# Merge gates ahead of the units in seven products of quarters, token-major projections, FoX heads begun after q and k

## The chip, the cores and the metric

One core of a Trainium2 chip runs the whole layer. The metric is the device time of one execution in microseconds, median of the runs. The engines are TensorE (matmuls and transposes, PE in the profile), VectorE (DVE), ScalarE (ACT), GpSimd (POOL) and SyncE (SP), which issues most DMAs.

## What is computed

The layer takes 512 tokens of width 2048 (float32) through an RMS norm and one wide input product, two branches, and a gated merge:

```
h = rmsnorm(x, norm_gain)
u = h @ w_in                                    # 2048 -> 12488 columns
q, k, v, z_a, f_logit | r, kr, vr, z_b, w, a | g_a, g_b = split(u)
o_a = fox_attention(q, k, v, cumsum(log_sigmoid(f_logit + bias))) * silu(z_a)   # 8 heads of 128
o_b = (rwkv7(shifted r, kr, vr, w, a) + bonus) * silu(z_b)                      # 16 heads of 64
m   = sigmoid(g_a) * (o_a @ w_proj_fox) + sigmoid(g_b) * (o_b @ w_proj_rwkv)    # 1024 -> 2048 each
out = rmsnorm(x + m @ w_out, final_norm_gain)
```

The two gates g_a and g_b are 2 x 2048 of the columns of u. The matrix products must hold float32 accuracy.

## The kernel before

Every large product is made of three matmuls in the float32r type: each operand is split into a high part (a cast, on ScalarE) and a low part (what the cast left, a subtraction on VectorE), and high x high, high x low and low x high are added up in PSUM. The normed input is kept transposed, as `hhi` and `hlo`, 16 blocks of 128 channels by 512 tokens.

`u_tile` (L292) makes one tile of 128 columns of u by 512 tokens: `product` (L278) runs over 16 blocks of 128 input channels, with a 128x128 piece of the weights stationary and 512 tokens moving, 48 matmuls in all. The weights come in pieces of 256 KB: `load_raw` (L236) issues the load on SyncE into one of four `raw` buffers, `split_pieces` (L254) makes `whi` (L266, ScalarE) and `wlo` (L267, VectorE), `next_piece` (L242) keeps both ahead of the matmuls. All pieces stand in one list in the order of use.

TensorE and SyncE run in the order in which the code emits; the other engines are ordered by the framework's scheduler from priorities. The order on TensorE comes from a main generator (`stage1`, L855) that emits the weight tiles, and workers that it spawns (`fox_head`, `rwkv_front`, `rwkv_chain` and others): after each matmul of the main generator a virtual clock in `mm` (L127) advances, and workers whose due time has come (the table `LAG`) put their small matmuls in between. So heads and chains of the recurrence ride in the gaps of the weight tiles.

The stages are, in time: the norm and the transposed input with the first tile `wd` (to 35 us), `ad` (to 47 us), the units (60 tiles, 47 to 897 us: per pair of RWKV heads the tiles k, r, z, v, each evacuated by `shift`, L443, and from the second pair on one FoX head with q, k, v, z and `fox_head`, L776), then the merge: 32 gate tiles `g` and 32 projection tiles `p` (24 matmuls each), with `p` three tiles behind `g`, and FoX head 7 between the first three `g` and the first `p` (L317 to L330, L910 to L942). The gate goes through a tanh on ScalarE into one of four `sg` buffers; after the projection VectorE forms (tanh + 1) x p and adds the second branch's product to the first's in `m_all`. `mhi` and `mlo` (L945 to L947) are its parts, channel-major, and serve the out stage (L1003 on) as stationary operand with 512 columns of w_out moving. The branches' outputs go through DRAM (`oa_d`, `ob_d`) and come back as `oraw`.

## Time and profile before

| | |
|---|---|
| median of 3 runs | 1675.99 us (1674.42 to 1678.16) |
| the profiled execution | 1676.68 us |
| its span | 1674.8 us |
| mean granted TensorE clock | 0.993 |
| TensorE busy | 1628.9 us (97%), 8506 instructions |
| VectorE busy | 958.0 us (57%) |
| ScalarE busy | 710.4 us (42%) |
| GpSimd busy | 83.6 us (5%) |
| DMA | 170.24 MB, mean 102 GB/s |

The busy time of an engine is the union of its instructions; matmuls overlap, so the 0.39 us of one matmul is its latency, and the distance from one start to the next is its price on the engine. The table is of one execution; the stretches below tell where in it an engine was busy.

### The profile page before, as it was taken

The numbers are of one execution on the slowest core, as the hardware profiler recorded it, in microseconds if no ns is written. First come the engines' busy times: TensorE is split into PE (matmuls) and PEld (weight loads), VectorE is DVE, ScalarE is ACT, GpSimd is POOL, SyncE is SP. The second block draws the span as 40 slices with busy tenths as digits, with TensorE's granted clock in tenths as the row PEclk, the third lists the DMA queues.
The fourth block names the chain that finished last, engine by engine and source line by source line (L and its number), as shares of the span: only waits on it lengthen the run. The fifth ranks groups of instructions, "written<-read, shape, count | busy, mean of one in ns | idle before, by whom it ended". The sixth has DMA issues, their size and how long they took to land.

```text
span 1674.8 us, 23424 instructions
## 1 busy us (share of the span) xinstructions
PE 1628.9 (97%) x8506; PEld 1332.3 (80%) x8506; DVE 958.0 (57%) x2005; ACT 710.4 (42%) x1453; POOL 83.6 (5%) x149
## 2 busy tenths in 40 slices
PE   6998998999999999999999999999999999999998
PEld 6887876778878778788788788888888888888886
DVE  6468587786877777678668454222224333353432
ACT  7544354474464464553744444222223222243322
POOL 3010001000000000010000000000000000001110
PEclk9999998999999999999999999999999999999999
DMA  5342423333333324334334244335334333343422
GB/s 167 97 107 69 105 61 90 98 87 86 90 96 98 99 70 111 86 78 104 85 86 115 76 123 118 95 98 148 94 96 148 97 95 98 98 160 117 138 83 101
DMA packets 287978, 170.24 MB, mean 102 GB/s; under 512 B 38790, under 2 KB 270830, under 8 KB 287222
## 3 DMA queue, kind: packets, MB, share of 16 engines
q1 hardware_dynamic: 284358, 156.13, 35.4%
q0 software_dynamic: 2064, 9.46, 1.5%
q10 hardware_dynamic: 1440, 3.15, 0.5%
q8 instruction: 67, 1.10, 0.3%
q14 instruction: 49, 0.40, 0.1%
HBM read 158.19 MB, written 10.50 MB: 101 GB/s over the span
## 4 chain that ended last, share of the span: by engine, by line
PE 83%; DVE 9%; ACT 3%; issue 2%; DMA 2%; SPq 1%; POOL 0%; DVEq 0%; ACTq 0%; POOLq 0%
PE u_g L135 20%; PE p L135 11%; PE o L135 10%; PE u_fq L135 6%; PE u_fk L135 5%; PE u_z L135 4%; PE u_fv L135 4%; PE u_k L135 4%; PE u_fz L135 4%; PE u_v L135 4%; PE u_r L135 2%; DVE Wt L482 2%; DVE W L642 1%; PE sc L135 1%; PE y L135 1%
## 5 line engine op out<-in xcount | busy, mean ns | idle before, releaser
L135 PE MATMUL u_g<-hhi,wlo_g 128*128 128x512 f32 x512 | 200.6, 392 | 0.0
L135 PE MATMUL u_g<-hhi,whi_g 128*128 128x512 f32 x512 | 200.4, 391 | 0.0
L135 PE MATMUL u_g<-hlo,whi_g 128*128 128x512 f32 x512 | 200.0, 391 | 0.0
L267 DVE TENSOR_TENSOR wlo_g<-raw_g,whi_g 128x512 fp32r<-128x512 f32 x128 | 88.4, 690 | 169.8 <-ACT whi_g L266 167.6
L266 ACT ACTIVATE whi_g<-raw_g 128x512 fp32r<-128x512 f32 x128 | 80.9, 632 | 228.1 <-PE u_g L135 115.1
L135 PEld LDWEIGHTS u_g<-hlo,whi_g 128*128 128x128 f32 x512 | 96.2, 188 | 20.3
L135 PEld LDWEIGHTS u_g<-hhi,wlo_g 128*128 128x128 f32 x512 | 96.2, 188 | 20.2
L135 PEld LDWEIGHTS u_g<-hhi,whi_g 128*128 128x128 f32 x512 | 96.2, 188 | 19.7
L482 DVE TENSOR_TENSOR Wt<-W,Lt 128x16 f32<-128x16 f32 (+30 forms) x248 | 101.0, 407 | 5.6
L267 DVE TENSOR_TENSOR wlo_p<-raw_p,whi_p 128x512 fp32r<-128x512 f32 x64 | 44.3, 693 | 103.3 <-ACT whi_p L266 103.3
L135 PE MATMUL p<-ohi,whi_p 128*128 128x512 f32 x256 | 101.0, 394 | 0.0
L135 PE MATMUL p<-ohi,wlo_p 128*128 128x512 f32 x256 | 100.4, 392 | 0.0
L135 PE MATMUL p<-olo,whi_p 128*128 128x512 f32 x256 | 99.6, 389 | 0.0
L266 ACT ACTIVATE whi_p<-raw_p 128x512 fp32r<-128x512 f32 x64 | 40.4, 631 | 121.9 <-PE u_g L135 120.3
L135 PE MATMUL o<-whi_o,mhi 128*128 128x512 f32 x224 | 87.3, 390 | 0.1
L135 PE MATMUL o<-wlo_o,mhi 128*128 128x512 f32 x224 | 87.2, 389 | 0.0
L135 PE MATMUL o<-whi_o,mlo 128*128 128x512 f32 x224 | 87.1, 389 | 0.0
L267 DVE TENSOR_TENSOR wlo_o<-raw_o,whi_o 128x512 fp32r<-128x512 f32 x56 | 42.6, 762 | 76.2 <-ACT whi_o L266 75.9
L642 DVE TENSOR_REDUCE W<-Wt 128x8 f32<-128x16 f32 (+30 forms) x248 | 72.4, 292 | 5.6
L266 ACT ACTIVATE whi_o<-raw_o 128x512 fp32r<-128x512 f32 x56 | 35.3, 631 | 83.6 <-PE o L135 79.3
L135 PE MATMUL u_fq<-hhi,whi_fq 128*128 128x512 f32 x128 | 53.7, 419 | 5.2 <-DVE z L448 5.2
L719 ACT ACTIVATE pre<-SV,E 64x64 f32<-64x64 f32 x112 | 38.6, 345 | 46.3 <-DVE SV L732 45.4
(352 smaller groups left out, 3924.3 us busy)
## 6 DMA issues: line engine op xcount, KB each, us to landing
raw_g<-in_w_in_dram SPq DMA_DIRECT2D x128, 256.0 KB
raw_o<-in_w_out_dram SPq DMA_DIRECT2D x56, 256.0 KB
raw_k<-in_w_in_dram SPq DMA_DIRECT2D x32, 256.0 KB
raw_r<-in_w_in_dram SPq DMA_DIRECT2D x32, 256.0 KB
raw_z<-in_w_in_dram SPq DMA_DIRECT2D x32, 256.0 KB
raw_v<-in_w_in_dram SPq DMA_DIRECT2D x32, 256.0 KB
raw_fq<-in_w_in_dram SPq DMA_DIRECT2D x32, 256.0 KB
raw_fk<-in_w_in_dram SPq DMA_DIRECT2D x32, 256.0 KB
```

The source lines that it names most:

```text
L135: PE.matmul(out, lhsT=lhsT, rhs=rhs, start=start, stop=stop, **kw)
L266: S.activation(whi, raw, AF.Copy)
L267: V.tensor_tensor(wlo, raw, whi.bitcast(F32), ALU.subtract)
L482: eng.tensor_tensor(o, a, b, op)
L642: V.tensor_reduce(W[:, :, i], tmp[:, :, 0:i + 1], AX.X, ALU.add)
L719: S.activation(pre[hs[q]], SV[hs[q], c, q, :], AF.Copy, scale=E1[hs[q], c, CH:CH + 1])
```

## The change

The two gates are computed first, right behind the tile `ad`, and for all tokens: in four groups of 1024 columns (two per gate). A group is a product of the 512 x 2048 input with a 2048 x 1024 block of weights. Each is cut into four quarters, and seven products of sums of quarters take the place of eight products of quarters, as in Strassen's method in Winograd's form (`fast`). Products are now token-major: a 128 x 128 piece of the input or of one of four sums of its quarters is stationary and 512 columns of weights move. A group has 28 units (seven products by four blocks of 256 rows) of 12 matmuls, and each unit needs a weight operand of 128 x 1024. VectorE forms the weight differences (`prep`), and the sums of the products from PSUM; ScalarE casts and takes the tanh; the result is stored by GpSimd's queue in `sg_d` in DRAM, 2 x 512 x 2048. In the first group, products that need no sums come first (`seq0`), and `make_sums` builds the four sums of the input's quarters beside them, in four rounds with one buffer `st`: GpSimd adds high and low parts to get the quarter back, VectorE makes the sums and low parts, ScalarE the casts. Weight loads are 512 KB, in four buffers `gb`, on SyncE. The pools of this stage are closed before those of the units open.

The tiles of the units come in the order of `order`: k and r of a pair, then the four tiles of a FoX head, then z and v of the pair. A FoX head begins behind its k tile and takes v and z when they come; head 7 follows head 6. One entry of `LAG` (f5) goes from 16.0 to 12.5.

The projections come behind all units. They too are token-major: for each branch and each block of 512 columns, four banks (one per 128 tokens), eight pieces of weights moving. The gates are read back from `sg_d` (four loads of 256 KB per block). The merged rows are then token-major, so `turn_merged` turns them by 64 transposes on TensorE, in sets of four: a block of columns is turned during the next block of the second branch, the last one behind the last matmul. The out stage is the same.

```diff
-    units = [("rw", 0), ("rw", 1)]
-    for i in range(2, 8):
-        units += [("fox", i - 2), ("rw", i)]
-    units += [("fox", 6)]
...
-    for n in range(len(merge) + WIN):
-        if n == WIN:
-            add_unit("fox", 7)
-        if n < len(merge):
-            br, j, g0, wp = merge[n]
-            add_tile(f"g{br}_{j}", [(0, w_in[:, g0 + j * P:g0 + (j + 1) * P])])
-        if n >= WIN:
-            br, j, g0, wp = merge[n - WIN]
-            add_tile(f"p{br}_{j}", [(0, wp[:, j * P:(j + 1) * P])], nk=FW // P)
...
+    order = []
+    for i in range(NP):
+        order += [("rw", i, "k"), ("rw", i, "r")]
+        if i > 1:
+            order += [("fox", i - 2, nm) for nm in "qkvz"]
+        order += [("rw", i, "z"), ("rw", i, "v")]
+    order += [("fox", i, nm) for i in (6, 7) for nm in "qkvz"]
...
+    for br, wp in enumerate((w_proj_rwkv[0], w_proj_fox[0])):
+        for n in range(4):
+            for k in range(KB):
+                pieces.append((f"p{br}_{n}_{k}", [(0, wp[k * P:(k + 1) * P, n * 512:(n + 1) * 512])], 1, 512))
...
+        seq0 = [(p, j) for p in "1256743" for j in J]
+        seq = [(p, j) for j in J for p in "15"] + [("6", j) for j in J] + [("2", 0)] + [("7", j) for j in J]
+        seq += [("2", 1), ("4", 0), ("2", 2), ("4", 1), ("2", 3), ("4", 2), ("4", 3)] + [("3", j) for j in J]
+        units = [(g, p, j) for g in groups for p, j in (seq0 if g == groups[0] else seq)]
+        of = {"1": ["11"], "2": ["21"], "3": ["22"], "4": [], "5": ["12"], "6": ["22"], "7": ["11"]}
+        of0 = {**of, "4": ["21"], "5": ["11", "12"]}
...
+        def prep(n):
+            g, p, j = units[n]
+            if p == "5":
+                Ts[j] = src = wp.tile([P, 2, 512], F32, tag="T", bufs=4, name=f"{name}T{g}{j}")
+                tt(V, src, raw[j, "12"], raw[j, "11"], ALU.subtract)
+            elif p == "6":
+                src = Ts[j]
+                tt(V, src, raw[j, "22"], src, ALU.subtract)
+            elif p == "7":
+                src = raw[j, "11"]
+                tt(V, src, Ts[j], src, ALU.subtract)
+            elif p == "4":
+                src = Ts[j]
+                tt(V, src, raw[j, "21"], src, ALU.subtract)
+            else:
+                src = raw[j, {"1": "11", "2": "21", "3": "22"}[p]]
+            hi = wp.tile([P, 2, 512], F32R, tag="hi", bufs=3, name=f"{name}h{g}{p}{j}")
+            lo = wp.tile([P, 2, 512], F32R, tag="lo", bufs=3, name=f"{name}l{g}{p}{j}")
+            S.activation(hi, src, AF.Copy)
+            tt(V, lo, src, hi.bitcast(F32), ALU.subtract)
+            ready[n] = (hi, lo)
...
+            for kk in range(2):
+                k = 2 * j + kk
+                for b in range(2):
+                    t = slice(b * P, (b + 1) * P)
+                    mm(ps[:, b, :], a_hi[:, k, t], w_hi[:, kk, :], start=begin and k == 0, stop=False,
+                       skip_group_check=True)
+                    yield
...
+            if p == "1":
+                s1 = ep.tile([P, 2, 512], F32, tag="ev", bufs=3, name=f"{name}s1{g}")
+                S.copy(s1, X)
+            elif p == "6":
+                u2 = ep.tile([P, 2, 512], F32, tag="ev", bufs=3, name=f"{name}u2{g}")
+                tt(V, u2, Y, s1, ALU.add)
+            elif p == "7":
+                u3 = ep.tile([P, 2, 512], F32, tag="ev", bufs=3, name=f"{name}u3{g}")
+                tt(V, u3, Y, s1, ALU.add)
+                tt(V, u3, Z, u3, ALU.add)
+                result(g, 1, 1, u3, u3)
+            elif p == "4":
+                tt(V, s1, Y, s1, ALU.add)
+                result(g, 1, 0, s1, s1)
+            elif p == "2":
+                c11 = ep.tile([P, 2, 512], F32, tag="ev", bufs=3, name=f"{name}c11{g}")
+                result(g, 0, 0, X, c11)
+            elif p == "3":
+                tt(V, u2, Z, u2, ALU.add)
+                result(g, 0, 1, u2, u2)
...
+    A = {p: [a[:, half[kb], tok[th]] for a in (hhi, hlo)] for p, th, kb in (("1", 0, 0), ("2", 0, 1), ("4", 1, 1))}
+    A |= {p: sums[s] for p, s in (("5", "s1"), ("6", "s2"), ("7", "s3"), ("3", "s4"))}
...
+        st = gw.tile([P, 4, 2, 256], F32, tag="st", name=f"st_{m}")
+        a11, a12, a21, a22 = (st[:, i] for i in range(4))
+        for a, th, kb in ((a21, 1, 0), (a22, 1, 1), (a11, 0, 0), (a12, 0, 1)):
+            k = slice(8 * kb + 2 * m, 8 * kb + 2 * m + 2)
+            tt(G, a, hhi[:, k, tok[th]].bitcast(F32), hlo[:, k, tok[th]].bitcast(F32), ALU.add)
+        s1, s3, s2, s4 = a22, a21, a11, a12
+        for s, dst, a, b, op in (("s1", s1, a21, a22, ALU.add), ("s3", s3, a11, a21, ALU.subtract),
+                                 ("s2", s2, s1, a11, ALU.subtract), ("s4", s4, a12, s2, ALU.subtract)):
+            tt(V, dst, a, b, op)
+            hi, lo = (t[:, 2 * m:2 * m + 2, :] for t in sums[s])
+            S.copy(hi, dst)
+            tt(V, lo, dst, hi.bitcast(F32), ALU.subtract)
...
+    def gate_result(g, th, cb, src, dst):
+        S.activation(dst, src, AF.Tanh, scale=0.5)
+        c0 = (g % 2) * 1024 + cb * 512
+        G.dma_start(sg_d[g // 2][th * 256:th * 256 + 256, c0:c0 + 512].rearrange("(b p) m -> p b m", p=P), dst)
...
+            for c in range(4):
+                k = 4 * n + c
+                pt = ps_ms(f"mT_{k}")
+                for t in range(4):
+                    tr(pt[:, t * P:(t + 1) * P], ms_[n][:, t, c * P:(c + 1) * P])
+                S.activation(mhi[:, k, :], pt, AF.Copy, scale=0.5)
+                V.scalar_tensor_tensor(mlo[:, k, :], pt, 0.5, mhi[:, k, :].bitcast(F32), ALU.mult, ALU.subtract)
+                yield
...
+                    for t in range(4):
+                        ts = slice(t * P, (t + 1) * P)
+                        mm(pss[t], ohi[:, ts], whi[:, 0, :], start=(k == 0), stop=False)
+                        yield
+                        mm(pss[t], ohi[:, ts], wlo[:, 0, :], start=False, stop=False)
+                        yield
+                        mm(pss[t], olo[:, ts], whi[:, 0, :], start=False, stop=(k == KB - 1))
+                        yield
+                    if br == 1 and n > 0 and k == 4:
+                        yield from turn_merged(n - 1)
+                m = ms_[n]
+                for t in range(4):
+                    sg = sgs.pop((br, n, t))
+                    if br == 0:
+                        V.scalar_tensor_tensor(m[:, t, :], sg, 1.0, pss[t], ALU.add, ALU.mult)
+                    else:
+                        V.scalar_tensor_tensor(sg, sg, 1.0, pss[t], ALU.add, ALU.mult)
+                        tt(V, m[:, t, :], m[:, t, :], sg, ALU.add)
+        yield from turn_merged(3)
```

On GpSimd the buffer `st` of the sums appears (its numbered names are the four rounds; `low` is the former fx, fa, fo, fc; `gc`, `gu`, `gs` are gate results). Before, at this place of GpSimd's order, behind the casts of the first weights:

```order
L407 MEMSET vT 128x64
L410 MEMSET E_0_483 128x8
L410 MEMSET E_1_484 128x8
L413 MEMSET DT_487 128x1024 [waits DMAHW3_49,DMAHW2_49,DMAHW4_49,DMAHW1_49,DMAHW5_49,DMAHW0_49,DMAHW6_49,DVE_49,DMAHW7_49,PE_49,Activation_49]
L413 MEMSET DT_488 128x1024
```

After:

```order
L470 TENSOR_TENSOR st_583<-hhi,hlo 128x512 [waits DVE_49,Activation_49] x4
L459 MEMSET low_478 8x512 [waits Pool_49]
L463 DMA c_dram<-low_479 8x512 [waits DVE_49]
L470 TENSOR_TENSOR st_640<-hhi,hlo 128x512 [waits DVE_49,Pool_49]
L470 TENSOR_TENSOR st_640<-hhi,hlo 128x512 x3
L470 TENSOR_TENSOR st_695<-hhi,hlo 128x512 [waits DVE_49]
L470 TENSOR_TENSOR st_695<-hhi,hlo 128x512 x3
L470 TENSOR_TENSOR st_752<-hhi,hlo 128x512 [waits DVE_49]
```

The first add of each later round waits for a VectorE instruction, the one that reads `st` last in the round before (s4l).

On VectorE, behind the first tiles, before:

```order
L426 TENSOR_TENSOR wdl<-wd,wdh 96x512 [waits DVE_49,Activation_49]
L471 SCALAR_TENSOR_TENSOR fx<-fx,fa 8x512 [waits Activation_49]
L267 TENSOR_TENSOR wlo_k_8_641<-raw_k_8_595,whi_k_8_640 128x512 [waits DMAHW1_49,PE_49,Activation_49]
L475 SCALAR_TENSOR_TENSOR fc<-fo,fx 8x512 [waits DVE_49,Pool_49]
L267 TENSOR_TENSOR wlo_k_12_659<-raw_k_12_613,whi_k_12_658 128x512 [waits DMAHW2_49,PE_49,Activation_49]
L448 SCALAR_TENSOR_TENSOR ad<-u_ad,par1m,ad 96x511 [waits Activation_49]
```

After, the end of the third round of sums and the begin of the fourth (`gl` is the low part of a weight operand, `gT` a weight difference, s1l to s4l low parts of the sums; gl_776 is the first of product 5):

```order
L470 TENSOR_TENSOR s2l<-st_695,s2h 128x512 [waits Activation_49]
L470 TENSOR_TENSOR st_695<-st_695 128x512 [waits Pool_49]
L470 TENSOR_TENSOR gl_717<-gb_21_657,gh_716 128x1024 [waits DMAHW5_49,PE_49,Activation_49]
L470 TENSOR_TENSOR gl_737<-gb_21_675,gh_736 128x1024 [waits DMAHW6_49,Activation_49]
L470 TENSOR_TENSOR s4l<-st_695,s4h 128x512 [waits Activation_49]
L470 TENSOR_TENSOR gT_773<-gb_12_714,gb_11_712 128x1024 [waits DMAHW7_49,DMAHW0_49]
L470 TENSOR_TENSOR st_752<-st_752 128x512 [waits DVE_49,Pool_49] x2
L470 TENSOR_TENSOR gl_776<-gT_773,gh_775 128x1024 [waits Activation_49]
```

The weight work of the gates now stands in one row with the sums, and product 5's first operand behind the first sums of the last round.

On TensorE, between the last projection and the out stage, before:

```order
L135 MATMUL p_15_13499<-ohi_7_12010,whi_p_15_4_13481 128x512
L135 MATMUL p_15_13499<-olo_7_12012,whi_p_15_4_13481 128x512
L135 MATMUL p_15_13499<-ohi_7_12010,wlo_p_15_4_13482 128x512
L135 MATMUL o_0_13589<-whi_o_0_13502,mhi 128x512 [waits DVE_49,Activation_49]
L135 MATMUL o_0_13589<-wlo_o_0_13503,mhi 128x512
```

After (`mT` is the bank of a set of four transposes):

```order
L150 MATMUL p_3_3_13356<-whi_p_3_7_13477,olo_7_12793 128x512
L154 MATMUL mT_13537<-ident,m_12029 128x128 [waits DVE_49,PE_49]
L154 MATMUL mT_13537<-ident,m_12029 128x128 [waits DVE_49] x3
L154 MATMUL mT_13544<-ident,m_12029 128x128 [waits PE_49]
L154 MATMUL mT_13544<-ident,m_12029 128x128 x3
L154 MATMUL mT_13551<-ident,m_12029 128x128 [waits PE_49]
L154 MATMUL mT_13551<-ident,m_12029 128x128 x3
L154 MATMUL mT_13558<-ident,m_12029 128x128 [waits DVE_49]
L154 MATMUL mT_13558<-ident,m_12029 128x128 x3
L150 MATMUL o_0_13582<-whi_o_0_13495,mhi 128x512 [waits Activation_49]
```

Four sets of transposes, which wait for VectorE, stand between the last projection matmul and the first of the out stage.

## Rows read from the trace of the kernel before

**Rows 1.** Busy time by stretches of the span.

```profile
core 0: us, PE busy (x) PEld busy (x) DVE busy (x) ACT busy (x) POOL busy (x), PEclk, DMA share, GB/s
0.00:20.00 20.00, 7.67 (x40) 7.31 (x41) 9.06 (x24) 12.55 (x26) 9.64 (x22) 1.00 0.85 254
...
100.00:200.00 100.00, 95.38 (x521) 77.33 (x521) 70.26 (x147) 39.06 (x77) 5.39 (x4) 0.97 0.36 91
200.00:300.00 100.00, 92.37 (x572) 74.34 (x568) 79.94 (x193) 51.26 (x120) 6.24 (x8) 0.95 0.32 79
1100.00:1200.00 100.00, 100.00 (x439) 82.23 (x438) 29.23 (x43) 26.32 (x43) 0.00 (x0) 1.00 0.44 119
```

**Rows 2.** Waits of TensorE: waited for, total, times, longest.

```profile
PE gp L135 <- DVE A L658: 6.7, 2, 6.6
...
PE u_fq L135 <- DVE z L448: 5.2, 2, 4.5
```

**Rows 3.** Timeline of TensorE, one gate tile: first, last, next tile.

```profile
1080.82 0.40 PE L135 MATMUL u_g<-hhi,whi_g 128*128 128x512 f32 x1
...
1091.53 0.39 PE L135 MATMUL u_g<-hhi,wlo_g 128*128 128x512 f32 x1
1091.75 0.40 PE L135 MATMUL p<-ohi,whi_p 128*128 128x512 f32 x1
```

**Rows 4.** Costliest groups of the page: one of three gate rows.

```profile
L135 PE MATMUL u_g<-hhi,wlo_g 128*128 128x512 f32 x512 | 200.6, 392 | 0.0
```

**Rows 5.** Groups by shape, VectorE and ScalarE: count, busy, mean ns.

```profile
L267 DVE TENSOR_TENSOR wlo_g<-raw_g,whi_g 128x512 fp32r<-128x512 f32 x128 | 88.4, 690 | 169.8 <-ACT whi_g L266 167.6 <-PE p L135 2.0
...
L482 DVE TENSOR_TENSOR pr<-pr,cmask 128x128 f32<-128x128 f32 x32 | 8.8, 288 | 0.4
...
L482 DVE TENSOR_TENSOR AR<-r,E 128x512 f32<-128x512 f32 x8 | 6.2, 769 | 0.0
...
L266 ACT ACTIVATE whi_g<-raw_g 128x512 fp32r<-128x512 f32 x128 | 80.9, 632 | 228.1 <-PE u_g L135 115.1 <-PE p L135 99.1 <-PE u_fz L135 10.4
```

**Rows 6.** Groups by shape, GpSimd.

```profile
L482 POOL TENSOR_TENSOR xo<-xo,gain 128x512 f32<-128x512 f32 x12 | 18.3, 1554 | 113.5 <-ACT fj L985 74.7 <-issue 38.9
L482 POOL TENSOR_TENSOR kn<-kn,a 128x512 f32<-128x512 f32 x8 | 12.7, 1589 | 43.4 <-DVE AR L545 43.4
```

**Rows 7.** Timelines of VectorE and TensorE near 47 us.

```profile
36.33 0.56 DVE L267 TENSOR_TENSOR wlo_ad<-raw_ad,whi_ad 128x384 fp32r<-128x384 f32 x1 [0.55 <-ACT whi_ad L266]
...
49.90 0.74 DVE L448 SCALAR_TENSOR_TENSOR ad<-u_ad,par1m,ad 96x511 f32<-96x511 f32 x1
...
46.66 0.40 PE L135 MATMUL u_ad<-hhi,wlo_ad 128*96 128x512 f32 x1
46.89 0.39 PE L135 MATMUL u_k<-hhi,whi_k 128*128 128x512 f32 x1
```

**Rows 8.** Timelines of GpSimd, VectorE and TensorE around two waits.

```profile
140.51 1.84 POOL L482 TENSOR_TENSOR kn<-kn,a 128x512 f32<-128x512 f32 x1 [5.99 <-DVE AR L545]
...
266.55 2.15 POOL L482 TENSOR_TENSOR kn<-kn,a 128x512 f32<-128x512 f32 x1 [5.33 <-DVE AR L545]
...
141.32 1.59 DVE L482 TENSOR_TENSOR AR<-r,E 128x512 f32<-128x512 f32 x1
...
146.53 0.77 PE L135 MATMUL u_fq<-hhi,whi_fq 128*128 128x512 f32 x1 [4.54 <-DVE z L448]
```

**Rows 9.** DMA issues: count, KB each, us to landing.

```profile
xo<-in_x_dram POOLq DMA_DIRECT2D x4, 1024.0 KB, 7.7
...
oa_d<-fz POOLq DMA_DIRECT2D x8, 256.0 KB, 2.3
ob_d<-y POOLq DMA_DIRECT2D x8, 256.0 KB, 2.8
```

**Rows 10.** Timeline of TensorE, four transposes between two matmuls.

```profile
912.53 0.39 PE L135 MATMUL u_g<-hhi,whi_g 128*128 128x512 f32 x1
912.76 0.60 PE L139 MATMUL bt<-ident,BK 128*128 128x128 f32 x4
913.11 0.48 PE L135 MATMUL u_g<-hlo,whi_g 128*128 128x512 f32 x1
913.43 0.39 PE L135 MATMUL u_g<-hhi,wlo_g 128*128 128x512 f32 x1
```

More of the change, by code (lines that the diff above doesn't have):

```diff
@@ L27 @@
 FW = 1024
+KB = 8
 RW0 = 4 * FW + NH
@@ L167, in hybrid_layer @@
     G.dma_start(grow, norm_gain.rearrange("o (r c) -> (o r) c", c=P))
-    xts = [xpool.tile([P, D], F32, tag="xt", bufs=4, name=f"x_{tb}") for tb in range(4)]
+    xts = [spool.tile([P, D], F32, tag=t, name=f"x_{tb}") for tb, t in enumerate(("s4h", "s4l", "s3h", "s3l"))]
     def load_x(eng, tb, hf):
```

436 lines of the change are left out of this document (255 added, 181 removed).

## The prediction

> **What bounds the kernel now.** I read the busy time by stretches first. The first columns are the stretch, its length and then each engine's busy time. In the gates-and-projections stretch at 1100 us TensorE is busy all of the 100 us, with 439 matmuls; VectorE is there busy 29 [rows 1]. The two stretches behind the first 20 us that fall short most are 100 to 200 and 200 to 300 us (95.4 and 92.4 us, granted clock 0.97 and 0.95 of the upper level, 2.4 GHz). So the end is set by the number of matmuls, and next by the few waits of TensorE: the waits list holds only small ones, of which `u_fq` behind VectorE's `z` (4.5 us in one piece) and `gp` behind `A` (6.6 us) are the largest inside the kernel [rows 2]. A gate tile of 48 matmuls takes from 1080.82 to 1091.75, when the next tile begins [rows 3]: 10.93 / 48 = 0.2277 us per matmul of 512 columns, and in the middle of it 0.227 from start to start. I use 0.227. A change is worth matmuls taken away, less every new wait.
>
> **What is removed.** The gates are 1536 matmuls, three rows like the one in [rows 4]. Seven products for eight leave 4 groups x 28 units x 12 = 1344. Saved: 192 x 0.227 = **43.6 us**, all on TensorE's path. A unit of 12 is 2.73 us, a group 76.3 us.
>
> **What that costs VectorE.** Before, a gate piece was a cast on ScalarE and one subtraction of 512 elements (0.690 us) on VectorE. Now VectorE also forms the weight differences, and works on 1024 elements. That length isn't in the trace: 512 take 0.690 and 128 take 0.288 [rows 5], so 1.05 ns for each further element, and 1024 are 1.23 us by estimate (between 1.2 and 1.38, twice the 512). A later group has 28 subtractions, 16 differences and 5 results: 49 x 1.23 = 60 us of 76. VectorE was busy 29 of 100 us beside the gates of before [rows 1]; now it is at 79%.
>
> **The first group** is the term that decides. Beside the same weight work it makes the sums of the token quarters: in each of four rounds GpSimd adds hhi and hlo four times into one buffer `st`, VectorE makes four sums and four low parts from it, and the next round's first GpSimd add waits for the last of those, s4l (the order shows this wait). A GpSimd add of 512 takes 1.55 us [rows 6], so a round is 4 x 1.55 = 6.2 us of GpSimd and then, by VectorE's order, 8 x 0.69 + 2 x 1.23 = 8.0 us, one after the other. By the times of before the gates begin at 46.9 us, when `u_ad` ends [rows 7]; the first s4l stands behind the shift of `ad`, which ran at 49.90 [rows 7], so it is out at about 51.3. Then 51.3 + 6.2 + 8.0 + 6.2 + 8.0 + 6.2 = 85.9 is when the last round's four sums can begin; two short and one long instruction later, at 88.5, the first operand of product 5 is ready, which TensorE wants after eight units, at 68.7. Six short and three long ones later (96.3) comes its second, and at 101.2 its fourth. Product 5 ends at 103.9 and not at 46.9 + 12 x 2.73 = 79.7: 24 us late. The rest is paced by two long instructions per unit, 2.5 of 2.73 us, and keeps up, but twice TensorE waits for a result to be taken from the bank that it wants to go on with (u2 before product 7, u3 before product 4), about 2 us each. **28 us.** Bounds: without any wait for GpSimd, VectorE's queue up to that last operand (32 short, 17 long and 5.4 us of others from 36.3 us, [rows 7]) ends at 84.7, which is 8 late, 12 with the two results; with GpSimd and VectorE hindering each other (below) and longer passes, 40.
> Behind such a wait the matmuls run slower: the first one after the 4.5 us wait at 142 us took 0.77 us instead of 0.39 [rows 3, 8], and the stretch's mean clock is 0.97 [rows 1], 3 us in 100. **3 us** (1 to 5).
>
> GpSimd and VectorE can hinder each other: `kn` on GpSimd took 1.84 us at 140.51, and VectorE's `AR<-r,E`, issued beside it, 1.59 us [rows 8] where its mean is 0.77 [rows 5]. In the order VectorE has only one long instruction to do while GpSimd makes a round's adds, so I count this as 0 and up to 4 us by one such row (0.8 + 0.3) per round.
> The Trainium skill ("SBUF — State Buffer", section "Who interferes with whom") says that a VectorE instruction with two inputs in SBUF and a GpSimd instruction that reads SBUF lock each other out, and the later one waits for the whole of the other. The pair of rows agrees in kind, with 1.59 us for 0.77; by the rule taken whole, all 16 adds would cost something and the sum would be that of rival (d).
>
> **The later groups.** Each needs 24 loads of 512 KB, one per 3.2 us, into four buffers. A load of 256 KB landed 2.3 to 2.8 us after issue and one of 1024 KB after 7.7 [rows 9], so 512 KB are 4 to 5 us, within the four buffers' lead. The rate with the results' stores is (12.6 + 2.1 MB) / 76 us = 190 GB/s; before it was about 100 there, and 254 in the opening 20 us [rows 1]. With VectorE at 79% in uneven order I take **7 us** for three groups (0 to 27). Behind the last gate matmul the first weights of the units need a cast and a subtraction, 0.63 + 0.69 [rows 5]: **1.5 us** (1 to 4). The stores, ScalarE's tanh and read-back lie beside TensorE's work, 0.
>
> **The units.** The same tiles in another order. The 4.5 us wait came from a tile that needs the bank which `z` of pair 1 leaves late; now `u_k2` comes in that place, behind the same two tiles, so the wait stays under another name. FoX q and k come before the pair's z and v, and the last FoX heads cover the last chain as gates did. **0** (-14 to +8).
>
> **The projections.** The 768 matmuls stay, now with the tokens stationary. The merged rows must be turned: 64 transposes in 16 sets. A set of four `bt` pushed the next matmul but one from +0.46 to +0.90 us [rows 10], 0.44 us: 16 x 0.44 = **7 us** (before, this was no TensorE work at all). The fourth set of a turn waits for the first of three banks to be emptied by ScalarE and VectorE, about 1 us in three turns, and in the second branch VectorE takes its results in pairs (two products, two sums, a weight part, two products), which hands over the third and fourth bank some 1.1 us late, at three changes of columns: **6 us** (2 to 9). At the end TensorE can't go on to the out stage until VectorE's last product and sum (4.3 us after the last matmul by that order), and the turn's emptying, 1.5 more: **6 us** (4 to 9). Before, the change from `p` to `o` had no wait worth a row.
>
> **Sum.** -43.6 + 28 + 3 + 7 + 1.5 + 0 + 7 + 6 + 6 = +14.9. Against the profiled execution, 1676.7 us, that is 1691.6; the median of the runs is 0.7 below that execution, so **1691 us**.
>
> **Rivals.**
> (a) It ends faster: the first group hardly waits. Place: product 5; mechanism: VectorE's sums aren't in line with GpSimd's adds, because rounds overlap more than the order suggests or GpSimd's adds are shorter. Then the 28 + 3 become 12 and the later groups' 7 become 0: 1691 - 19 - 7 = 1665. It decides for "faster" once all waits of the gates are under 25 us (the 39.5 in my sum less the 14.9 by which it is slower). For it: VectorE's total work allows it. Against: the wait on s4l is in the order. Chance 0.2.
> (b) The units win: with gates gone ahead, the new order gets back what 100 to 300 us lose (4.6 + 7.6 us of idle and about 8 of clock in [rows 1]) and some of the later 2 us per stretch. With 14 of it, 1677, with 20, 1671. Against: the same tiles stand in front of the same waits. Chance 0.15.
> (c) The later groups fall to the pace of loads or of VectorE: at 1.38 us per long instruction VectorE needs 68 us, and with a load of 7.7 us four buffers give one per 1.9 us only if each is freed at once. Price 20 more, 1711. For it: 190 GB/s is near twice what the kernel drew. Chance 0.12.
> (d) The lock between GpSimd and VectorE counts: 4 to 10 more, from 0.6 us (`kn` at 2.15 for 1.55 at 266.55, [rows 8]) for each of 16 adds: 1695 to 1701. Chance 0.1.
> My own sum, 1680 to 1700: 0.43.
>
> **Numbers.** A difference of 0.2% (3.4 us) is about what a measurement of this kernel can tell. Faster: 0.17 of (a), 0.1 of (b), 0.03 from my sum's low edge = 0.3. Same: 0.02 + 0.03 + 0.05 = 0.1. Slower: 0.6. The range 1662 to 1708 leaves out most of (c) and the far ends of (a) and (b), 0.2 together.
>
> **What would show it.** In the profile after: TensorE waiting for VectorE's low part `gl` (or ScalarE's `gh`) some 20 us around 70 to 95 us, with GpSimd and VectorE taking turns on `st`; the first group ending near 150 us; later groups 76 to 80 us each; the first `u_k` near 392 us; a wait of 4 to 5 us in the units under `u_k`; transposes `mT` near the end with a wait for VectorE. I'm wrong if the first group ends before 135 us, if groups take over 85 us, or if the stage of the units differs by more than 10 us from its 850.

## The result, and the profile after

The changed kernel takes **1713.0 us** (median of 4 runs, 1712.9 to 1719.2) where the kernel before takes 1675.2 on the same chip: a ratio of 1.023, 95% interval 1.0205 to 1.0259. It is slower, as forecast, but by 37.8 us where the sum said 14.9, and it ends 5 us above the range. The profiled execution is one of 1712.98 us with a span of 1711.3, 36.5 us longer than the span before.

The page of the changed kernel: busy times, TensorE's rows of the 40 slices, and the chain:

```profile
PE 1614.6 (94%) x8378; PEld 1310.4 (77%) x8378; DVE 1121.3 (66%) x2105; ACT 759.8 (44%) x1440; POOL 123.2 (7%) x181
...
PE   5789999999989989899999999999999999999998
...
PEclk9899999999999999999999999999999999999999
...
PE 68%; DVE 18%; DMA 6%; issue 3%; ACT 3%; POOL 1%; SPq 0%; DVEq 0%; ACTq 0%; POOLq 0%
```

TensorE is still busy nearly always, but it holds only 68% of the chain, and VectorE 18%. The slices in which it falls short are the first three, up to 128 us, with a dip of the granted clock in the second (43 to 86 us).

Where the time went is read from TensorE's timeline at the borders of the stages. Before, gates, units and projections were mixed, so there the gates are 1536 matmuls at 0.2277 us, the price in the tile of [rows 3], and the units are what is left. The projections before are 768 matmuls at 0.2296 us. That price is read from one projection tile of 24 matmuls in TensorE's timeline of the kernel before, its first matmul and the first of the next tile:

```profile
1305.47 0.40 PE L135 MATMUL p<-ohi,whi_p 128*128 128x512 f32 x1
...
1310.98 0.40 PE L135 MATMUL u_g<-hhi,whi_g 128*128 128x512 f32 x1
```

| stage | before, us | after, us | difference | my sum |
|---|---|---|---|---|
| start to the end of `u_ad` | 47.1 | 51.3 | +4.2 | 0 |
| gates, to the first `u_k` | 349.7 | 345.0 | -4.7 | -4.1 |
| units, with head 7's last matmuls | 919.1 | 928.2 | +9.1 | 0 |
| projections and transposes | 176.3 | 203.8 | +27.5 | +19 |
| out | 175.3 | 175.4 | +0.1 | 0 |

The 3.3 us of head 7 that lie between the projections' matmuls are counted to the units; from the first `u_k` to the first `p` it is 924.9 us, and from there to the first `o` 207.1, and these two lengths are used below. So the gates, where nearly all my working was, came out as a whole as said: the 192 matmuls saved 43.6 us, and the 345.0 us are 39.9 more than 1344 x 0.227, which waits and slow matmuls took back (39.5 in the sum). The miss lies in the rows of the start, the units and the projections.

**The gates.** By stretches, the beginning of the first group and the first of the three later ones:

```profile
core 0: us, PE busy (x) PEld busy (x) DVE busy (x) ACT busy (x) POOL busy (x), PEclk, DMA share, GB/s
51.15:60.00 8.85, 8.55 (x38) 6.76 (x36) 6.70 (x7) 4.67 (x8) 5.04 (x4) 1.00 0.40 118
60.00:70.00 10.00, 4.35 (x11) 3.15 (x11) 9.81 (x11) 5.29 (x7) 3.36 (x3) 0.83 0.25 60
70.00:80.00 10.00, 6.47 (x25) 4.65 (x25) 7.49 (x8) 4.39 (x7) 5.29 (x4) 0.92 0.30 97
80.00:90.00 10.00, 8.06 (x24) 6.11 (x24) 7.49 (x8) 2.77 (x4) 6.38 (x4) 0.74 0.65 210
90.00:100.00 10.00, 6.39 (x19) 4.53 (x20) 8.15 (x10) 4.97 (x6) 0.77 (x1) 0.77 0.66 195
100.00:110.00 10.00, 10.00 (x40) 8.15 (x40) 9.66 (x9) 4.25 (x4) 0.00 (x0) 0.89 0.88 287
...
154.80:233.70 78.90, 77.46 (x337) 62.73 (x337) 56.58 (x49) 34.51 (x33) 2.86 (x4) 1.00 0.61 182
```

The column to follow is the count behind PE: 38 matmuls in the first 8.85 us, then 11, 25, 24 and 19 in ten each, then 40. VectorE is nearly full (9.81 of 10) or hands over to GpSimd (5.29 and 6.38 on POOL). Where TensorE has stood, the granted clock is 0.74 to 0.92, so that even the 10.00 us of busy time at 100 hold only 40 matmuls. The first group lasts from 51.15 to 154.8, 103.6 us for 76.3 us of matmuls.

VectorE and GpSimd take turns on `st` as the order had shown. Timeline of both, the end of round three and the begin of round four of the sums:

```profile
81.92 6.38 POOL L470 TENSOR_TENSOR st<-hhi,hlo 128x512 f32<-128x512 f32 x4 [6.64 <-DVE s4l L470]
...
78.29 0.69 DVE L470 TENSOR_TENSOR st<-st 128x512 f32<-128x512 f32 x1
...
81.16 0.69 DVE L470 TENSOR_TENSOR s4l<-st,s4h 128x512 fp32r<-128x512 f32 x1
...
85.39 3.46 DVE L470 TENSOR_TENSOR st<-st 128x512 f32<-128x512 f32 x2 [2.41 <-POOL st L470]
```

GpSimd's four adds wait 6.64 us for `s4l` (the row at 81.16 in the last round), VectorE's next sums wait 2.41 us for the adds. And the first two sums, which start at 85.39 while GpSimd's adds go on until 88.30, take 3.46 us together; one of them alone takes 0.69 (row at 78.29). In the two rounds before, three such sums took 4.14 and 4.20 us, beside the adds too, so the excess is 2.1 us in each of these rounds.

**The projections.** TensorE's waits from the first projection matmul to the first of the out stage, then pieces of its timeline: the start, an undisturbed stretch, the wait at a turn, and the end:

```profile
PE mT L154 <- DVE m L470: 3.1, 4, 2.1
PE mT L154 <- DVE mlo L1121: 2.8, 3, 1.3
PE p L150 <- DVE sg L1153: 2.5, 3, 0.8
PE p L150 <- DVE fz L1039: 2.0, 1, 2.0
PE p L150 <- ACT whi_p L296: 1.1, 1, 1.1
```

```profile
1323.89 0.57 PE L150 MATMUL p<-whi_p,ohi 128*128 128x512 f32 x1 [1.98 <-DVE fz L1039]
...
1327.65 0.40 PE L150 MATMUL p<-whi_p,ohi 128*128 128x512 f32 x1
...
1430.22 0.39 PE L150 MATMUL p<-whi_p,ohi 128*128 128x512 f32 x1
...
1430.91 0.40 PE L150 MATMUL p<-whi_p,ohi 128*128 128x512 f32 x1
...
1459.96 0.66 PE L154 MATMUL mT<-ident,m 128*128 128x128 f32 x4 [1.28 <-DVE mlo L1121]
...
1524.92 0.33 PE L154 MATMUL mT<-ident,m 128*128 128x128 f32 x1 [2.07 <-DVE m L470]
...
1528.20 0.78 PE L150 MATMUL o<-whi_o,mhi 128*128 128x512 f32 x1
```

Three things are there that my working doesn't have. The fourth matmul of the stage waits 1.98 us for a bank that `u_fz` of head 7 still holds, and the nine matmuls from 1323.89 to 1327.65 come every 0.42 us. Undisturbed, three matmuls take 0.70 us or a shade less (1430.22 to 1430.91), 0.2333 each, where one took 0.2296 before and the sum had 0.227: times 768, 2.8 us more than before. And a wait of 1.1 us for weights (`whi_p`) stands at 1363. Ahead of it GpSimd's queue issues two loads of 1 MB for the out stage:

```profile
1351.45 0.54 POOL L1167 DMA_DIRECT2D gain<-in_final_norm_gain_dram  x1
1355.70 0.54 POOL L1171 DMA_DIRECT2D xo<-in_x_dram  x1 [3.71 <-DMA oa_d<-fz]
```

From 1355 to 1365 us the DMA engines are busy 0.91 and 0.88 of the time.

**The start.** Timelines of ScalarE and TensorE in the changed kernel, then of TensorE in the kernel before:

```profile
15.39 0.30 ACT L417 CAST bones<-ones 128x128 fp32r<-128x128 f32 x1 [4.02 <-POOL ones L416]
...
17.44 0.69 PE L154 MATMUL xT<-ident,x 128*128 128x128 f32 x2 [8.17 <-DVE x L233]
```

```profile
13.05 0.47 PE L139 MATMUL xT<-ident,x 128*128 128x128 f32 x1 [4.01 <-DVE x L213]
```

The cast of the matrix of ones waits 4.02 us for GpSimd's fills, and the norm of the second half of the input stands behind it on ScalarE. TensorE waits 8.17 us for the rows, where it waited 4.01 before, and goes on 4.4 us later.

### The profile page after: what moved, and what is told of

Same layout as the page of the kernel before. It is cut to its first block, busy times and chain, and to the rows that moved or that the text cites. A ratio compares the mean times of both kernels' runs of the same rounds, so it can differ in the third digit from the quotient of the medians.

```text
span 1711.3 us, 23236 instructions
## 1 busy us (share of the span) xinstructions
PE 1614.6 (94%) x8378; PEld 1310.4 (77%) x8378; DVE 1121.3 (66%) x2105; ACT 759.8 (44%) x1440; POOL 123.2 (7%) x181
## 4 chain that ended last, share of the span: by engine, by line
PE 68%; DVE 18%; DMA 6%; issue 3%; ACT 3%; POOL 1%; SPq 0%; DVEq 0%; ACTq 0%; POOLq 0%
PE o L150 10%; PE p L150 8%; PE gY L150 7%; PE u_r L150 5%; PE u_fv L150 4%; PE u_k L150 4%; PE u_z L150 4%; PE u_fq L150 4%; PE u_fk L150 4%; DMA gb<-in_w_in_dram 4%; PE u_fz L150 4%; DVE Wt L470 3%; PE u_v L150 3%; DVE W L824 2%; PE gX L150 2%
## 5 line engine op out<-in xcount | busy, mean ns | idle before, releaser
L150 PE MATMUL p<-whi_p,ohi 128*128 128x512 f32 x256 | 102.5, 400 | 5.6 <-DVE sg L1153 2.5
L150 PE MATMUL p<-wlo_p,ohi 128*128 128x512 f32 x256 | 102.0, 399 | 0.2 <-DVE wlo_p L297 0.2
L150 PE MATMUL p<-whi_p,olo 128*128 128x512 f32 x256 | 102.1, 399 | 0.0
L528 ACT ACTIVATE gh<-gb 128x1024 fp32r<-128x1024 f32 x64 | 67.7, 1060 | 76.7 <-PE gY L150 50.5
L470 DVE TENSOR_TENSOR gl<-gb,gh 128x1024 fp32r<-128x1024 f32 x64 | 77.9, 1220 | 26.9 <-ACT gh L528 26.8
L528 ACT ACTIVATE gh<-gT 128x1024 fp32r<-128x1024 f32 x48 | 50.7, 1059 | 68.6 <-PE gY L150 22.6
L470 DVE TENSOR_TENSOR gl<-gT,gh 128x1024 fp32r<-128x1024 f32 x48 | 58.3, 1221 | 13.0 <-ACT gh L528 13.0
L150 PEld LDWEIGHTS p<-whi_p,ohi 128*128 128x128 f32 x256 | 48.5, 189 | 19.2 <-DVE sg L1153 3.8
L150 PE MATMUL gX<-gl,hhi 128*128 128x512 f32 x128 | 52.4, 409 | 10.0 <-DVE gl L470 10.0
L150 PE MATMUL u_k<-hhi,whi_k 128*128 128x512 f32 x128 | 53.3, 416 | 7.5 <-DVE z L433 4.5
```

The lines of the kernel that those rows point to most:

```text
L150: PE.matmul(out, lhsT=lhsT, rhs=rhs, start=start, stop=stop, **kw)
L470: eng.tensor_tensor(o, a, b, op)
L528: S.activation(hi, src, AF.Copy)
```

## The experiments

All single times of one profiled run, unless said otherwise, beside runs of the kernel before on the same chip (1672.7 to 1675.0 us); the changed kernel is 1713.0. It was not run again beside them, so differences of 2 or 3 us in a whole time say nothing, and the runs are read by stages. Even a stage that an edit doesn't touch moves: the projections are between 205.8 and 211.3 us long in `e1`, `e4`, `e5`, `e6`, `e7` and `e8`.

**The start: ones built later** (`e1_late_ones`). The block of line 412 is moved behind the gates:

```diff
-    bones = const.tile([P, P], F32R, name="bones")
-    ones2 = gw.tile([P, 2, T], F32, tag="ev", bufs=3, name="ones2")[:, 0, 0:P]
...
-    S.copy(bones, ones2)
...
+    S.copy(bones, ones2)
+
     delta = rw.tile([P, 8, 32], mybir.dt.bfloat16, name="delta")
```

> One edit: the block of ones (bones, a cast on ScalarE behind three GpSimd memsets) is built where the kernel before built it, with the units' constants, and not ahead of the gates. Theory A: in the changed kernel this cast stands on ScalarE ahead of the second rows' norm and waits 4.0 us for GpSimd, so the first transposes of the second rows come 4 us late (17.4 for 13.05 us); here u_ad ends near 47.1 and not at 51.3, and the whole is 3.5 to 4.5 us shorter (1709). Rival B: the loads of x are late because x now shares buffers with the sums; then u_ad still ends at 51 and the time stays at 1713.

1713.2 us, not the 1709 of theory A, and yet its reason for the late start is right. `u_ad` ends at 47.4 instead of 51.3. TensorE's row at the start, and one of its waits in the projections:

```profile
13.12 0.69 PE L154 MATMUL xT<-ident,x 128*128 128x128 f32 x2 [3.76 <-DVE x L233]
```

```profile
PE p L150 <- ACT whi_p L296: 3.4, 2, 2.3
```

The rows of the input are waited for until 13.12; gates (345.1) and units (925.0) are as long as in the changed kernel. The 3.8 us are lost again in the projections, 211.2 us instead of 207.1: there TensorE now waits 3.4 us for `whi_p` where it waited 1.1, and the matmuls behind that wait come every 0.42 us, 1.6 us more. What makes those weights late is open. The gates' read-back, four loads of 256 KB for each block, is on the same queue as the weights, but it stands ahead of them at every block. The longest such wait comes at one place only, 12 to 17 us behind the issue of `gain`, in the changed kernel and in seven of the runs; in `e7_old_units`, where `gain` goes out 29 us earlier in the stage, the wait comes 24 us earlier. In `e3_no_turn` there is none, though `gain` and `xo` are loaded. So these two loads are the likelier cause, beside the read-back, and no run moves the one without the other.

**What the transposes cost** (`e3_no_turn`):

```diff
-                pt = ps_ms(f"mT_{k}")
-                for t in range(4):
-                    tr(pt[:, t * P:(t + 1) * P], ms_[n][:, t, c * P:(c + 1) * P])
+                pt = ms_[n][:, c, :]
```

> The 64 transposes of the merged rows are left out: ScalarE and VectorE make the same high and low parts, straight from the rows in SBUF (so the rows enter the out stage unturned). Theory A: the turns cost what the profile of the changed kernel shows, three times 3.0 to 3.4 us of TensorE (4 x 0.44 and the wait for the first bank) and 1 to 2 at the end, where VectorE is waited for in any case: the stage from the first p to the first o goes from 207 to 195 to 198 us. Rival B: with the transposes gone the same time is waited for VectorE's low parts; 203 to 207 us stay.

1695.8 us. From the first `p` to the first `o` it is 191.1 us, 16.0 less, more than theory A had, and TensorE goes on to the out stage without a wait. The 16.0 hold 1.1 us for `whi_p`, which isn't waited for in this run, and they don't hold the 2.5 us at changes of columns (`sg`), which are still there. So my three terms for turns, banks and the end (7 + 6 + 6 = 19) stand against 16.0 - 1.1 + 2.5 = 17.4 and are about right together. The other 14.8 us of the stage (191.1 - 176.3) have nothing to do with the transposes: 3.3 of head 7, 2.8 from the spacing, 3.7 at the first bank and 2.5 at column changes make 12.3, and 2.5 have no name.

**Is it the place of the stationary operand?** (`e2_low_operands`) The first branch's operands are put in a big tile that is free by then, at 15 to 48 KB of a partition, the second branch's stay at 180 to 213 KB:

```diff
+            low = hpool.tile([P, KC, T], F32R, tag="hi", name="low_o") if br == 0 else None
...
-                hi = mg.tile([P, T], F32R, tag="osp", bufs=16, name=f"ohi_{br}_{i}")
+                hi = low[:, i, :] if br == 0 else mg.tile([P, T], F32R, tag="osp", bufs=16, name=f"ohi_{br}_{i}")
```

> One edit: in the first branch's projections the high and low parts of the branch's output stand in the buffer of hhi (SBUF addresses 15 to 48 KB per partition), not in the merge pool (from 180 KB on); the second branch stays as it is. In the changed kernel a projection matmul starts every 0.2333 us and a matmul of the out stage, of the same form, every 0.2267. Theory A: the place of the stationary operand in SBUF makes the difference; the first branch's 384 matmuls go at 0.227 (2.5 us less), the second branch's stay at 0.233, and the copies, which now wait for the last unit tile, cost 1 to 3 us at the start of the projections: 1711 to 1714 in all. Rival B: it is the projections' loads or banks; then both branches stay at 0.233.

1717.7 us, 3.7 above the upper end of theory A. TensorE's timeline in the first branch, then in the second:

```profile
1390.04 0.39 PE L150 MATMUL p<-wlo_p,low_o 128*128 128x512 f32 x1
...
1390.72 0.39 PE L150 MATMUL p<-wlo_p,low_o 128*128 128x512 f32 x1
...
1439.72 0.40 PE L150 MATMUL p<-wlo_p,ohi 128*128 128x512 f32 x1
...
1440.42 0.39 PE L150 MATMUL p<-wlo_p,ohi 128*128 128x512 f32 x1
```

0.68 against 0.70 us for three. The weights move from the same buffers in both branches, and in the changed kernel both branches have 0.70, so the place of the stationary operand makes this difference. The 2.6 us for one branch are eaten by waits: the big tile is free only when the last units have read it (1.47 and 0.95 us at the first matmuls), and TensorE waits 3.3 us for `whi_p` where it waited 1.1.

**GpSimd's adds left out** (`e4_no_gpsimd`). The sums are made from the high parts alone:

```diff
-            tt(G, a, hhi[:, k, tok[th]].bitcast(F32), hlo[:, k, tok[th]].bitcast(F32), ALU.add)
+            src[id(a)] = hhi[:, k, tok[th]].bitcast(F32)
```

> The sums of the token quarters are made from the high parts alone: the 16 GpSimd adds that put high and low parts together are left out, VectorE's and ScalarE's work is the same. Theory A: the rounds GpSimd, VectorE, GpSimd through the one buffer st hold the first group; without GpSimd VectorE's own queue decides, product 5 ends near 92 us and not at 107.7, the first group near 139 and not at 154.8, 16 us less in all (1697). Rival B: VectorE's amount of work alone holds it; the first group gains under 5 us.

1703.2 us; the first group takes 94.0 us instead of 103.6. By stretches:

```profile
60.00:70.00 10.00, 7.77 (x26) 5.95 (x27) 9.96 (x16) 6.70 (x10) 0.00 (x0) 0.83 0.51 157
70.00:80.00 10.00, 7.79 (x35) 6.12 (x33) 9.62 (x13) 5.33 (x7) 0.00 (x0) 1.00 0.44 125
80.00:90.00 10.00, 8.06 (x27) 6.28 (x28) 5.58 (x5) 3.13 (x4) 0.76 (x1) 0.83 1.00 339
```

Product 5 ends at 95.5 us, 92 by theory A. So of the 27.4 us lost in this group, GpSimd's adds carry 9.6. The rest stays: VectorE alone fills 9.96 and 9.62 of 10 us, and then, at product 5, the loads take over (the DMA engines busy all of the ten, 339 GB/s; VectorE's weight difference at 89.14 waits 2.07 us for its load). The truth lies between the two theories.

**More time for the sums** (`e6_pairs`). The first two groups share products 1 and 2, so that TensorE has twice the work that needs no sums. The sums begin at units 0, 3, 6 and 9, not 0, 2, 4 and 6, and the second group, like the first, now loads 32 quarters of 512 KB where it loaded 24:

```diff
+        units = [(g, p, j) for p in "12" for g in two for j in J] + [(g, p, j) for g in two for p in "56743" for j in J]
```

> Products 1 and 2 of the first two groups come first (16 units that need no sums), the second group's pair of banks for them is one of the Z banks; then products 5, 6, 7, 4, 3 of each of the two groups; one more buffer for results. Nothing is left out. Theory A: the sums have 16 units instead of 8 before product 5 needs them, so the rounds are over when they are wanted: the first two groups take 160 to 165 us (56 units x 2.72 = 152.3, and 8 to 12 of waits) where they took 182.6; 18 to 22 us less in all (1691 to 1695). Rival B: VectorE's total in two groups decides; waits only move to later products, less than 10 us gained.

1715.8 us: the two groups take 185.2 us, and 182.6 in the changed kernel. TensorE's waits in them only have other places:

```profile
PE gX L150 <- DVE gl L470: 11.3, 4, 5.0
PE gY L150 <- DVE gu L470: 6.5, 4, 2.1
```

Theory A falls, and with it the reading that only time is lacking. The four waits for `gl` stand in products 1 and 2, which need no sums. VectorE's timeline before the second of them, which ends at 77.18 us:

```profile
72.55 3.44 DVE L470 TENSOR_TENSOR st<-st 128x512 f32<-128x512 f32 x2 [2.65 <-POOL st L470]
75.92 1.21 DVE L470 TENSOR_TENSOR gl<-gb,gh 128x1024 fp32r<-128x1024 f32 x1
```

The weight part `gl` stands behind sums that wait 2.65 us for GpSimd and then take 3.44 us for 1.38. The first and the third wait have the same rows before them; before the fourth VectorE waits 4.26 us for a load. So with the sums ahead of the weights on VectorE the waits come earlier and don't go away. The eight loads more are in the second group, so that group can't be compared.

**Fewer loads** (`e5_fewer_loads`). In the later groups product 5 takes no quarter of its own, 20 loads for 24:

```diff
-        of = {"1": ["11"], "2": ["21"], "3": ["22"], "4": [], "5": ["12"], "6": ["22"], "7": ["11"]}
+        of = {"1": ["11"], "2": ["21"], "3": ["22"], "4": [], "5": [], "6": ["22"], "7": ["11"]}
```

> In the three later groups the load of the quarter for product 5 is left out (its difference is formed from the quarter that is there), 20 loads of 512 KB for 24 in a group and 12 for 16 behind the group's start; every engine's work is the same. Theory A: the 2.8 to 3.5 us that a later group takes beyond 28 x 2.72 = 76.2 us are waits for loads (260 GB/s there, share of the DMA engines 0.8): groups of 76.2 to 77.2 us, 7 to 9 us less in all (1704 to 1706). Rival B: VectorE's order makes them; groups of 79 us stay and the time is within 2 us of 1713.

1708.7 us. By stretches, the first later group:

```profile
154.70:231.10 76.40, 76.40 (x338) 62.84 (x336) 55.95 (x49) 34.52 (x33) 2.85 (x4) 1.00 0.53 163
```

76.4, 77.3 and 77.3 us instead of 78.9, 79.7 and 79.8, with VectorE as busy as ever (55.95 us, 56.58 in the changed kernel). That is 7.4 us; the whole is only 4.3 shorter, since the projections take 209.3 us here and the rest up to the end 0.9 more. The later groups' waits are late loads; VectorE, though busy 57 of 79 us, isn't what they wait for in the end.

**The units in the order of before** (`e7_old_units`):

```diff
-    for i in range(NP):
-        order += [("rw", i, "k"), ("rw", i, "r")]
-        if i > 1:
-            order += [("fox", i - 2, nm) for nm in "qkvz"]
-        order += [("rw", i, "z"), ("rw", i, "v")]
+    order = [("rw", i, nm) for i in (0, 1) for nm in "krzv"]
+    for i in range(2, NP):
+        order += [("fox", i - 2, nm) for nm in "qkvz"] + [("rw", i, nm) for nm in "krzv"]
```

> One edit: the tiles of the units in the order of the kernel before (k, r, z, v of a pair together, a FoX head's four tiles behind them); heads still begin behind their k tile. Theory A: the order of the tiles moves waits but is worth nothing (0, -14 to +8 in the prediction); the units take 922 to 928 us where they took 925. Rival B: the shifted order is worth something; then they take 930 or more.

1742.6 us; the units take 951.3 us and not 924.9. Three of TensorE's waits in them:

```profile
PE p L150 <- ACT ohi L1098: 8.3, 1, 8.3
PE fpt L154 <- ACT pr L979: 7.6, 5, 2.2
...
PE u_fq L150 <- DVE z L430: 4.5, 1, 4.5
```

With heads that begin behind k, and no gates behind the units, the new order of tiles is worth 26.4 us; without it the first projection waits 8.3 us for its operand, and the heads' own transposes 7.6. This isn't the price of the old units as a whole: in the kernel before a head begins behind its fourth tile, and f5 is 16.0, and no run has that without the gates behind the units. The wait behind `z`, 4.5 us, is under `u_fq` again; in the changed kernel the same 4.5 us stand under `u_k`, as foretold.

**A plain first group** (`e8_plain_first`), eight products with no sums, the sums made beside it for the later ones; the ones as in the first experiment:

```diff
+        seq0 = [(p, j) for p in "abcd" for j in J]
...
-        if n % 2 or n > 6:
+        if n not in (1, 4, 7, 10):
```

> Two edits: the ones as in e1_late_ones, and the first group as eight plain products of quarters (16 weight operands, each for all 512 tokens, 384 matmuls), while the sums for the later groups are made beside it; nothing is left out. Theory A: 48 matmuls more (10.9 us), but no wait for sums and 16 loads for 32: the first group takes 88 to 90 us and not 103.6, the start is 3.8 us earlier, 1693 to 1696 in all. Rival B: the waits move into the second group, whose product 5 is load-bound in the same way; less than 8 us gained beside the start's 3.8.

1702.8 us. The group has 48 matmuls (10.9 us) more and is 7.4 us shorter, 96.1 for 103.5 from its first matmul to the first of the next group. It isn't the 88 to 90 of the theory: TensorE waits 2.7 us for `gl0b`, which stands on VectorE behind a sum that waits 2.65 us for GpSimd, and 2.6 for the shift of `ad`, and 3.8 are slow matmuls. Rival B's waits in the second group aren't there: it takes 76.6 us, with all of its 24 loads, now that the group ahead of it needs 16 and not 32.

**Eight edits together** (`e9_combined`), of which only the first two had been run before: ones later, plain first group with its sums begun later, x and the sums in each other's place, the projections' first banks changed, the gates read back by GpSimd's queue, one set of transposes between two weight pieces with products ahead of sums in the second branch, the operands first in their pool, the last turn behind the first four pieces of the out stage.

```diff
-                nc.sync.dma_start(sg, sg_d[br][t * P:(t + 1) * P, n * 512:(n + 1) * 512])
+                G.dma_start(sg, sg_d[br][t * P:(t + 1) * P, n * 512:(n + 1) * 512])
...
-                    if br == 1 and n > 0 and k == 4:
-                        yield from turn_merged(n - 1)
+                    if br == 1 and n > 0 and k in (2, 3, 4, 5):
+                        yield from turn_merged(n - 1, (k - 2,))
```

> Eight edits on the changed kernel, nothing left out, read by stages. (1) the ones late as in e1: start -3.8 us. (2) the first group plain as in e8, its sums begun later (units 3, 6, 9, 12) so that weights go first: first group 88 to 91 us and not 96. (3) x and the sums change places in SBUF, so that the units' first weights stand where product 5's sums were and not where the last product's are: u_k starts under 1 us behind the last gate matmul and not 2.9. (4) the projections' first two banks are those that the last unit tile doesn't hold: no 2 us wait there. (5) gates read back on GpSimd's queue. (6) the transposes one set at a time over four row blocks, and VectorE takes four products ahead of four sums: no waits of 0.7 to 1.3 us at turns and changes of columns. (7) the branches' parts stand at 139 to 172 KB and not from 180 KB: a projection matmul every 0.227 us if the place in SBUF counts and its bound lies above (theory A), 0.233 if not. (8) four row blocks of the out stage ahead of the last turn: no wait of 3 us and more there. Projections 190 to 194 us for 207, 1668 to 1676 in all. Rival B: what is taken from one wait is waited for at the next (VectorE, loads): above 1685.

1686.9 us, 26.1 less than the changed kernel and 14.2 more than the kernel before on the same chip. That is above theory A's 1668 to 1676 and where rival B puts it. Projections and out stage are 367.4 us together, 15.1 less. In the projections the waits for `sg` and `whi_p` are gone, of that at the first bank 1.1 us is left and of those at the turns one of 1.2. The first group is 97 us, not 88 to 91, and 2.92 us are still waited before the first `u_k`. The matmuls of the projections still come every 0.2333 us, with the operands at 139 to 172 KB.

**Three more causes at once** (`e10_second`, 4 runs): the ones built on VectorE behind `u_ad`, the first group's weights ahead of the sums, and a branch's operands in one tile.

```diff
+        osp = mg.tile([P, 2, 8, T], F32R, name="osp")
...
+                hi = osp[:, 0, i, :]
...
+                with tc.high_priority(offset=HW if n < 16 else 0):
+                    prep(n + 2)
```

> The kernel e9_combined with three edits: the ones for the head sums built on VectorE directly behind the low-rank product (in e9_combined their cast held ScalarE for 7.47 us before the units), the weights' preparation of the first group set ahead of the sums, which start one unit later, and the operands of a branch in one tile of 32 KB, high parts 16 KB from their low parts (there: pairs of 2 KB side by side). e9_combined took 1686.9 us. Theory A (each of the three is the cause of what it stands beside): no wait of 2.92 before the first unit (-3), first group 90 for 97 us (-7), and the projections' matmuls one per 0.2267 us for 0.2333 (768 x 0.0067 = -5): 1672 us, within 0.3% of the kernel before. Theory B (the place of the operands in the memory is not what sets the 0.2333, and sums that come later only wait later): rate 0.2333 as it was, first group 95 to 97: 1682 to 1687 us.

1694.1 us, 1.012 times the kernel before (1.010 to 1.013), so the three edits together didn't help: it took 7 us more than the kernel it started from. None of what theory A named shows as a cause, the wait before the first unit is as long as it was, the first group takes 99.5 us and the spacing is the same; theory B's time was too low as well. Timelines of ScalarE, TensorE, GpSimd and VectorE:

```profile
385.03 1.06 ACT L644 ACTIVATE gu<-gu 128x1024 f32<-128x1024 f32 x1 [8.31 <-DVE gu L465]
385.99 2.17 ACT L297 ACTIVATE whi_k<-raw_k 128x512 fp32r<-128x512 f32 x4
...
74.37 6.46 POOL L465 TENSOR_TENSOR st<-hhi,hlo 128x512 f32<-128x512 f32 x4 [5.73 <-DVE s4l L465]
...
74.56 2.18 DVE L465 TENSOR_TENSOR gl0b<-gb,gh0b 128x1024 fp32r<-128x1024 f32 x1 [0.27 <-ACT gh0b L530]
```

Two of its readings are of use. The wait before the first `u_k` is 2.92 us with the ones out of the way too: on ScalarE the last gate's tanh (`gu`), which waits 8.31 us for its sum, stands ahead of the cast of the units' first weights. No run changed that order. And the weight part `gl0b`, now put beside GpSimd's adds, takes 2.18 us for 1.22: what VectorE does early it does beside GpSimd's adds, and slower.

## Why the prediction was wrong in size

Of the 21.3 us by which the sum was short of the 36.2 in the table, 9.1 lie in the units, which the sum had at 0, 8.5 in the projections and 4.2 in the start, for which it had no term; the gates gave back 0.6.

**Right, step by step.** The 192 matmuls are gone. A VectorE instruction of 1024 elements takes 1.22 us (estimate 1.23). Product 5 of the first group ended at 107.7 us, by my schedule of rounds at 103.9 and, with the start 4.2 us later, 108.1. Later groups take 78.9 to 79.8 us, 9.7 more than their matmuls in all (I had 7), and the loads are the reason. (The rows of 256 KB in [rows 9], which I took for loads, are stores.) The 4.5 us wait went under `u_k`. Before the first `u_k` TensorE waits 2.9 us, within the bounds of 1 to 4, but for ScalarE, which stands at the last gate's tanh.

**Right in sum, not in parts: the first group.** I had 28 for waits and 3 for the clock. TensorE's nine waits there are 18.1 us and the remaining 9.2 are slow matmuls: 27.4. I had taken the clock's loss from a stretch of 100 us with one long wait; here seven of the nine waits, 15.0 us, lie between 60 and 97 us, and the granted clock is 0.74 to 0.92 from 60 to 110 us. The mechanism was also only a third of it: without GpSimd's adds 17.7 of the 27.4 us stay, which is the lower bound that I gave for VectorE's own queue (12, with 3 of clock) and little more. That the sum came out near 27.4 is therefore luck in part: I had the waits 10 us too long and the slow matmuls 6 too short. Rival (d), that GpSimd and VectorE slow each other, is real, 2.1 us in each of three rounds (3.46 for two sums of 0.69); it is in the 9.6 us that went with GpSimd's adds, and no run separates the two. The Trainium skill ("SBUF — State Buffer", section "Who interferes with whom") has the two engines lock each other out for whole instructions; the rows agree in kind, with 3.46 us for 1.38.

**Wrong: the projections**, 27.5 where I had 19. The step that failed is "The 768 matmuls stay": I priced what was added, and took it that the rest would cost what it had cost. The rows showed 0.2333 for 0.2296 (2.8 us), a first bank that the last unit still holds and the slow matmuls behind it (3.7), and weights that come late (1.4, cause open); 2.2 have no name. The terms that I had, at 17.4 for 19, were sound.

**Wrong: the start**, 4.2 us where I had nothing. The change builds the block of ones ahead of the gates, and I didn't follow what stood behind its cast on ScalarE; `e1_late_ones` shows that this is the cause.

**Wrong: the units**, +9.1 for 0, just outside the bounds (-14 to +8). The step that failed is that the same tiles in another order bring the same waits. From the first `u_k` to the last projection TensorE's waits were 24.3 us before; between 396.2 and 1321 us now they are 30.8, and the granted clock is 0.98 for 0.99. The rows that matter:

```profile
PE vt L154 <- DVE vT L433: 6.7, 4, 2.4
PE gp L150 <- DVE fst L981: 4.8, 1, 4.8
...
PE u_k L150 <- DVE z L433: 4.5, 1, 4.5
...
PE gp L150 <- DVE A L840: 4.1, 1, 4.1
```

The waits that were there went under other names; the two at `gp` (8.9 us) stand for 9.3 at `gp` before, of which [rows 2] has 6.7. New is `vt`, 6.7 us in four pieces: the transposes of v behind the shift of v, the tile with which a pair now ends. That is the size of the growth in waits; the rest, some 2.6 us, would be slow matmuls. No run tried an order that takes `vt` away, so this is a reading and not shown, and the cause stays open.

Rival (b) fell: with the new order the units are longer than in the kernel before, though it is worth 26.4 us beside heads that begin early. Rival (a) falls with the 27.4 us of the first group, rival (c) with later groups under 80 us.

## What to carry to other kernels

A product saved on the busiest engine is worth what its operands let it be: before counting matmuls, lay out the other engines' work up to the first operand that is late, and add the slow clock for all of the time in which TensorE stops and starts, not for one wait. When work is moved out of a stage, ask what it had covered there: a new order worth 26 us left the units here still 9 us longer than they were. And price the instructions that stay as carefully as the new ones: the spacing of 768 matmuls, the bank that the stage before still holds and weights that come late were 8 us together. And more time for a late operand didn't help here while VectorE had slow work ahead of it.

## What the runs showed of the hardware that I had not expected

- Matmuls of 512 columns with weights moving from the same buffers come every 0.2267 us with the stationary operand at 15 to 48 KB of a partition and every 0.2333 us with it at 139 to 172 or 180 to 213 KB. One tile or small ones, high and low parts side by side or 16 KB apart makes no difference between those. In the kernel before, where the parts at 180 to 213 KB moved and the weights were stationary, it was 0.2296. Why isn't settled.
- Two VectorE sums that ran beside GpSimd's adds took 3.46 us for 1.38, and one weight part 2.18 for 1.22.
- In the first group 18.1 us of waits, 15.0 of them between 60 and 97 us, came with 9.2 us of slow matmuls; behind one wait of 1.98 us at the start of the projections nine matmuls came every 0.42 us, 1.7 us more.
